# Order of work in the output projection, the gate/up products and the last rows of a decoder block on one core

## The chip, the cores and the metric

The kernel runs on one core of one Trainium2 chip. The metric is device time in microseconds for one launch, the median over the runs shown; lower is better.

## What is computed

The reference is one decoder layer on 1024 tokens of width 1024, in float32: RMSNorm, one projection, two attention branches merged by gates, an output projection, then a SwiGLU feed-forward of width 2816 and a last RMSNorm. The part that matters here, cut from it:

```
merged = (gates[:, :, 0] * (o_a @ w_branch_dsa[l])
          + gates[:, :, 1] * (o_b @ w_branch_diff[l]))
x = x + merged @ w_out[l]

h = rmsnorm(x, norm_ffn_g[l])
gu = h @ w_ffn_in[l]
x = x + (jax.nn.silu(gu[..., :D_FF]) * gu[..., D_FF:]) @ w_ffn_out[l]

return rmsnorm(x, norm_final_g)
```

## The kernel before

Every float32 product is made of three matmuls, with the operands split into a high and a low part (`PASS`: hi·hi, lo·hi, hi·lo). ScalarE (ACT) writes the high part, GpSimd (POOL) or VectorE (DVE) the low part (L101, L102).

**Output projection.** The merged activations come as eight chunks of 128 channels; the last chunk is finished by DVE and ACT just before the projection begins. `outp(q, i)` makes one block of 128 tokens by 256 columns: 24 matmuls (L968) over the eight chunks into a bank `mm`, of which there are two, and then DVE adds the bank to the token row `x2[i]` (L973), which was loaded from memory (L924) into a row tile of the pool `r4`. That pool opens after the pool of the branch stage has closed, on the same bytes.

**Gate and up products.** The 22 column groups f of 128 gate and 128 up channels are made by Strassen's scheme: seven products of 12 matmuls for each f, in the order A11, S2, A12, S3, S1, A22, S4 (`SEQ`). `load_f` brings a gate row and an up row of weights (L936). DVE builds S1 to S4 from them (L1043 to L1046); `prep` splits each operand four products ahead, the high part on ACT (`ahi`) and the low part on POOL (`alo`), with six buffers each. `product_out` takes the results out of the banks. S2, S3 and A22 collect in one bank `tr`: DVE copies out S2's sum (L1088) before S3 may add to it, and S3's (L1094) before A22 may. S4 has the bank `big` (L1105 takes it out, ACT applies SiLU at L1106, L1107 multiplies). After every odd f, `sums` makes four more DVE combinations of the pair (L1119 to L1122) for the down projection and stores them. On even f, `load_w` loads two rows of down weights; on odd f, `tsums` combines them on POOL (L1138 to L1141) and stores them (L1143). The passage from an odd f to the next f is called a seam below.

All loads and stores are issued by one queue, SP, in program order; each waits for its own condition, and what stands behind it waits too. The row tiles r0 to r15 are handed out from a list of free halves (`full`, `half_`), first freed first. The order on each engine is set by a scheduler at compile time, from the program's order and its own estimate of when operands are there; `keep_in_program_order` pins an instruction. Engines run their queues in that order.

**Last rows.** The last three units of the down projection are done row by row: DVE adds the bank to x2 (L1276), ACT squares, and `finish` makes the last norm of the row (L1240, L97, POOL's power at L98, then L1244 on ACT and L1245 on DVE) and stores it (L1247).

```
        product(n)
        prep(n + AHEAD)
        if j == 5:
            load_f(f + 2)
        if j == 3:
            if f % 2 == 0:
                load_w(f // 2)
            else:
                tsums(f // 2)
```

Of the kernel before, what the change touches and what calls it, by code (L numbers as in the profile page):

```python
# [22 lines left out]
KC = D // P  # L23
# [27 lines left out]
def block_kernel(ctx, tc, x, pos, g_mix, w_qk, w_v, q_scale, w_idx, w_gate, ikg, ikb, lams, sub_g, gate_b,  # L51
                 w_bdsa, w_bdiff, w_out, g_ffn, w_ffi, w_ffo, g_fin, out):
    nc = tc.nc
    V, A, G, T = nc.vector, nc.scalar, nc.gpsimd, nc.tensor
# [7 lines left out]
    def mm_bank():  # L62
        return ps.tile([P, 512], F32, name="mm")
# [36 lines left out]
    def split(hi, lo, src, lo_eng):  # L100
        A.activation(hi, src, AF.Copy)  # L101
        lo_eng.tensor_sub(lo, src, hi.bitcast(F32))  # L102
# [356 lines left out]
    for br in range(2):  # L459
        w0 = 8 * br  # L460
        for u in range(2):
            fetch(w0 + 2 + u)
            xx = []
            for c in range(2):
                pt = mm_bank()
# [16 lines left out]
        for c in range(2, 8):  # L482
            fetch(w0 + c + 2)
            for u in range(2):
                pt = mm_bank()
# [8 lines left out]
    for g in range(4):  # L494
        w0 = 16 + 2 * g
        for s in range(4):
            if s % 2 == 0:
                fetch(w0 + 2 + s // 2)
            pt = mm_bank().rearrange("p (a b) -> p a b", a=2)
            for tt in range(2):  # L500
                t = 2 * s + tt
                n = 0
# [298 lines left out]
    for m in range(8):  # L801
        prs = {}
        for j, t in enumerate(ORDER2):
# [6 lines left out]
            n = 8 * m + j  # L810
# [28 lines left out]
    with tc.tile_pool(name="mw", bufs=2) as mw:  # L839
        wot = {}  # L840

        def fetch_o(n, eng=G):
            if n < 8 and n not in wot:
                wot[n] = W3.get(w_out[n // 2, n % 2], eng)
# [25 lines left out]


    R4 = 16
    r4p = ctx.enter_context(tc.tile_pool(name="r4", bufs=1))
    r4p.tile([P, 32], F32, name="shift")
    rows_ = [r4p.tile([P, D], F32, name=f"r{j}") for j in range(R4)]
    b1p = ctx.enter_context(tc.tile_pool(name="b1", bufs=1))
# [1 line left out]
    class Space:  # L878
# [26 lines left out]
        def drop(self, *aps):  # L905
            for ap in aps:
                self.free += self.of.pop(id(ap))[1]
# [4 lines left out]
    def blk(early):  # L912
        if early:
            return b1p.tile([P, 2, 4, 512], F32R, name="blk", bufs=2)
        return b2p.tile([P, 2, 4, 512], F32R, name="blk", bufs=5)
# [16 lines left out]
    def load_f(f):  # L932
        if f < NF and f not in raws:
            raws[f] = [full() for _ in range(2)]
            for j, t in enumerate(raws[f]):
                nc.sync.dma_start(t, w_ffi[f + j * NF])  # L936
# [13 lines left out]
    def turn2(op, p_):  # L950

        pt = big_bank().rearrange("p u (c t) -> p u c t", c=4)
        for u in range(2):
            turn(pt[:, u], 0, tt[p_ + u][op])
        return pt

    def land2(op, p_, pt):
        sl = slice(p_ * P, p_ * P + 2 * P)
        hi, lo = (ops[op][:, a, :, sl].rearrange("p c (u t) -> p u c t", u=2) for a in range(2))
        split(hi, lo, pt, V)  # L960

    def outp(q, i):
        act = actA if i < 4 else actB
        pt = mm_bank()
        n = 0
        for k in range(KC):
            for a, b in PASS:
                T.matmul(pt[:, :256], lhsT=act[a][:, k, i % 4 * P:i % 4 * P + P],  # L968
                         rhs=wot[2 * q + k // 4][b][:, (k % 4) * 256:(k % 4) * 256 + 256],
                         start=n == 0, stop=n == 23)  # L970
                n += 1
        sl = slice(q * 256, q * 256 + 256)
        V.tensor_add(x2[i][:, sl], pt[:, :256], x2[i][:, sl])  # L973

# [18 lines left out]
        d["B22"] = sp4.second(hB)  # L993

    for q in range(2):
        for n in range(NT):
            outp(q, n)
            if q == 1 and n == 0:
                A.activation(small.tile([P, 1], F32, name="warm"), x2[0][:, 256:257], AF.Silu)
            if q == 1 and n in (1, 4):  # L1000
                fetch_o(4 + (n == 4))
# [5 lines left out]
    for n in range(NT + LAG + 1):  # L1007
        if n < NT:
            outp(2, n)
        if n >= LAG and n - LAG < NT:  # L1010
            i = n - LAG
            outp(3, i)
            rows(i)
        if n > LAG:
            i = n - LAG - 1
# [16 lines left out]
    def prep(n, early=False):  # L1032
        if n >= len(plan):
            return
        f, (a_, _, _) = plan[n]
        if f not in src_:
            g, u = raws[f]
            src_[f] = dict(A11=g[:, :512], A12=g[:, 512:], A22=u[:, 512:], own=[g, u])
        d = src_[f]
        if a_[0] == "S" and "S2" not in d:  # L1040
            S1, S2, S4 = (half_() for _ in range(3))
            S3 = u = d["own"][1][:, :512]
            V.tensor_add(S1, u, d["A22"])  # L1043
            V.tensor_sub(S2, S1, d["A11"])
            V.tensor_sub(S3, d["A11"], u)  # L1045
            V.tensor_sub(S4, d["A12"], S2)  # L1046
            d.update(S1=S1, S2=S2, S3=S3, S4=S4)
            d["own"] += [S1, S2, S4]
        if early:
            t = W3.pool.tile([P, 1024], F32R, name="raw", bufs=2)  # L1050
            hi, lo = t[:, :512], t[:, 512:]
        else:
            hi = arp.tile([P, 512], F32R, name="ahi", bufs=6)
            lo = arp.tile([P, 512], F32R, name="alo", bufs=6)
        split(hi, lo, d[a_], G)
        wops[n] = hi, lo
        if a_ == "S4":
            drop(*d["own"])
# [3 lines left out]
    def product(n):  # L1062
        product_mm(n)
        product_out(n)
# [64 lines left out]
    def load_w(j):  # L1129
        wrow[j] = [full() for _ in range(2)]  # L1130
        for q, t in enumerate(wrow[j]):
            tc.keep_in_program_order(nc.sync.dma_start(t, w_ffo[2 * j + q]))
# [34 lines left out]
    def split_u(n):  # L1167
        if n >= len(unit) or n in uop:
            return
        if n % 2 == 0:  # L1170
            ublk[n // 2] = blk(False).rearrange("p a b c -> p (a b c)").rearrange("p (n a c) -> p n a c", n=2, a=2)
        v = ublk[n // 2][:, n % 2]
        split(v[:, 0, :], v[:, 1, :], uraw[n], V)
        drop(uraw[n])
        uop[n] = v
# [18 lines left out]
    for n in range(2, len(plan)):  # L1194
        f, j = n // 7, n % 7
        if f == 0:
            for op in {2: ("T3",), 3: ("T1",), 4: ("T4",), 5: ("B22",)}.get(n, ()):
                ops[op] = blk(False)
                for p_ in (0, 2):
                    land2(op, p_, turn2(op, p_))  # L1200
                drop(*(tt[p_][op] for p_ in range(4)))
                if op == "T3":
                    load_f(1)
        product(n)
        prep(n + AHEAD)
        if j == 5:
            load_f(f + 2)
        if j == 3:
            if f % 2 == 0:
# [3 lines that stand above are left out]
        if f == NF - 1 and j:  # L1213
            for k in (0, 1):
                load_u(2 * j - 2 + k)
                if j > 1:
                    split_u(2 * j - 4 + k)
# [19 lines left out]

    def finish(i):
        sq = sqs[i]
        V.tensor_add(sq[:, 0:1], sq[:, 0:1], sq[:, 1:2])  # L1240
        r = small.tile([P, 1], F32, name="rstd")
        rsqrt(r, sq[:, 0:1], D, EPS)

        A.activation(x2[i][:, :512], x2[i][:, :512], AF.Copy, scale=r)  # L1244
        V.scalar_tensor_tensor(x2[i][:, 512:], x2[i][:, 512:], r, gfin[:, 512:], op0=OP.mult, op1=OP.mult)  # L1245
        for u in range(2):
            nc.sync.dma_start(out[i * P:(i + 1) * P, u * 512:u * 512 + 512], x2[i][:, u * 512:u * 512 + 512])  # L1247

    def evict(p, r, X):
        L, H = slice(0, 512), slice(512, 1024)  # L1250
        if p == 0:
            pA[r] = half_()
            A.activation(pA[r], X, AF.Copy)
        elif p == 1:
            V.tensor_add(x2[r][:, L], X, x2[r][:, L])
            square(r, 0)
            G.tensor_mul(x2[r][:, L], x2[r][:, L], gfin[:, L])
        elif p == 2:
            u2[r] = half_()
            V.tensor_add(u2[r], X, pA[r])  # L1260
            G.tensor_add(u2[r], u2[r], x2[r][:, H])
        elif p == 3:
            u3[r] = half_()
            V.tensor_add(u3[r], X, pA[r])
            G.tensor_add(u3[r], u3[r], x2[4 + r][:, H])
            G.tensor_add(pA[r], pA[r], x2[4 + r][:, L])
        elif p == 4:
            V.tensor_add(x2[4 + r][:, L], X, pA[r])
            square(4 + r, 0)
            G.tensor_mul(x2[4 + r][:, L], x2[4 + r][:, L], gfin[:, L])  # L1270
        elif p == 5:
            V.tensor_add(x2[4 + r][:, H], X, u3[r])
            square(4 + r, 1)
            finish(4 + r)
        else:
            V.tensor_add(x2[r][:, H], X, u2[r])  # L1276
            square(r, 1)
            finish(r)

    def bank_set(k):  # L1280
        if k:
# [16 lines left out]
    for n, (p, j) in enumerate(unit):  # L1298
        if j == 0 and p in OPEN:
            bs_ = bank_set(p == 2)  # L1300
        if n == 2:
            x2_load()
            gfin = row4(g_fin)
        if n < len(unit) - TAILU:
            for r in R:
                unit_mm(n, r)
                if j == NP - 1:
                    evict(p, r, bs_[r])
        elif n == len(unit) - TAILU:
            for r in R:  # L1310
                for m in range(n, len(unit)):
                    unit_mm(m, r)
                evict(p, r, bs_[r])
        split_u(n + SA)
        load_u(n + LA)

# [74 lines left out]
```

## Time and profile before

| | us |
|---|---|
| median of 3 runs (1617.27 to 1619.66) | 1617.34 |
| the profiled execution | 1619.83 |
| its span, first to last instruction | 1617.9 |
| TensorE (PE) busy in the span | 1548.1 |
| DVE busy | 1156.8 |
| ACT busy | 669.1 |
| POOL busy | 568.7 |

The span is that of the profiled execution alone; about 2 us lie outside it. PE, DVE, ACT, POOL and SP are the engines; "idle before, releaser" is how long an engine had nothing to do before an instruction and what ended that. The output projection runs from 843 to 944 us of the span, the gate and up products from 946 to 1395, the down projection from 1395 to 1608, the last rows to the end.

### The profile page before, as it was taken

What the parts mean: (1) busy time and instruction counts of PE and PEld (TensorE: products, weight loads), DVE (VectorE), ACT (ScalarE), POOL (GpSimd) and SP (SyncE); (2) the same over time, 40 slices, a digit from 0 to 9 for tenths busy, and PEclk for the clock granted to TensorE, in tenths of its full rate; (3) what the DMA queues carried; (4) which work ended last, traced back from release to release, by engine and by line L of the source; (5) the groups of instructions that cost most, each with busy time, mean ns of one, the idle gap of its engine ahead of it and who ended that gap; (6) DMA issues with size and microseconds to landing.
All of it is one profiled execution on the core that took longest, in us unless ns stands there. A gap on an engine that the chain in (4) does not pass through costs nothing. (4 is left out here: it accounts for less than half of the span.)

```text
span 1617.9 us, 22643 instructions
## 1 busy us (share of the span) xinstructions
PE 1548.1 (96%) x8204; PEld 1318.3 (81%) x8204; DVE 1156.8 (71%) x1880; ACT 669.1 (41%) x1199; POOL 568.7 (35%) x465
## 2 busy tenths in 40 slices
PE   7999999999999998999999989999999999999997
PEld 6788879998888787788779977788788878887886
DVE  6579999989999999788781486555555555755653
ACT  5454542231221888777730243233233223443343
POOL 2541611242220013322421136666566666203311
PEclk9999999999999999999999999999999999999999
DMA  5243243349421476774474133444344445885532
GB/s 174 86 146 128 88 148 107 111 141 245 137 89 40 105 152 161 186 197 144 153 260 170 53 110 130 149 163 166 133 169 163 159 150 195 315 316 178 166 130 104
DMA packets 108079, 247.45 MB, mean 153 GB/s; under 512 B 12480, under 2 KB 30016, under 8 KB 107968
## 3 DMA queue, kind: packets, MB, share of 16 engines
q1 hardware_dynamic: 107968, 246.02, 46.7%
q8 instruction: 64, 1.05, 0.3%
q14 instruction: 47, 0.39, 0.1%
HBM read 167.06 MB, written 78.91 MB: 152 GB/s over the span
## 5 line engine op out<-in xcount | busy, mean ns | idle before, releaser
L102 POOL TENSOR_TENSOR alo<-r,ahi 128x512 fp32r<-128x512 f32 x152 | 207.2, 1371 | 163.5 <-ACT ahi L101 147.7
L102 POOL TENSOR_TENSOR wlo<-raw,whi 128x1024 fp32r<-128x1024 f32 (+1 forms) x49 | 116.6, 2385 | 288.4 <-ACT whi L101 288.4
L101 ACT ACTIVATE ahi<-r 128x512 fp32r<-128x512 f32 x152 | 95.4, 631 | 260.3 <-PE big L1076 88.1
L1076 PE MATMUL tr<-blk,ahi 128*128 128x512 f32 x528 | 165.6, 394 | 8.0 <-DVE r L1088 7.3
L299 DVE MAX8 m<-score 128x8 f32<-128x640 f32 (+5 forms) x176 | 162.6, 924 | 5.4 <-POOL score L283 0.4
L300 DVE MATCH_REPLACE8 score<-m,score 128x640 f32<-128x640 f32 (+5 forms) x176 | 159.5, 906 | 0.0
L102 DVE TENSOR_TENSOR blk<-r,blk 128x1024 fp32r<-128x1024 f32 x77 | 101.7, 1353 | 73.7 <-ACT blk L101 73.2
L101 ACT ACTIVATE whi<-raw 128x1024 fp32r<-128x1024 f32 (+1 forms) x52 | 53.4, 1031 | 207.1 <-issue 110.2
L1076 PEld LDWEIGHTS tr<-blk,ahi 128*128 128x128 f32 x528 | 99.1, 189 | 32.6 <-DVE r L1088 10.7
L101 ACT ACTIVATE blk<-r 128x1024 fp32r<-128x1024 f32 x77 | 78.1, 1053 | 108.3 <-PE big L1292 44.4
L1076 PE MATMUL big<-blk,ahi 128*128 128x512 f32 x352 | 108.9, 390 | 0.9 <-DVE blk L102 0.9
L427 PE MATMUL mm<-hT_hi,whi 128*128 128x512 f32 x256 | 102.8, 401 | 3.3 <-DVE st_lo L489 2.3
L1076 PE MATMUL mm<-blk,ahi 128*128 128x512 f32 x336 | 104.3, 391 | 0.8 <-ACT r L1085 0.8
L1076 PE MATMUL tr<-blk,alo 128*128 128x512 f32 x264 | 103.7, 393 | 0.6 <-POOL alo L102 0.6
L427 PE MATMUL mm<-hT_lo,whi 128*128 128x512 f32 x256 | 101.2, 395 | 0.0
L427 PE MATMUL mm<-hT_hi,wlo 128*128 128x512 f32 x256 | 101.0, 394 | 0.0
L427 PE MATMUL big<-hT_hi,whi 128*128 128x512 f32 x256 | 99.6, 389 | 0.0
L427 PE MATMUL big<-hT_lo,whi 128*128 128x512 f32 x256 | 99.6, 389 | 0.0
L427 PE MATMUL big<-hT_hi,wlo 128*128 128x512 f32 x256 | 99.6, 389 | 0.0
L1292 PE MATMUL big<-blk 128*128 128x512 f32 x396 | 91.8, 391 | 1.9 <-DVE r L1260 1.5
L1292 PEld LDWEIGHTS big<-blk 128*128 128x128 f32 x396 | 73.8, 188 | 19.5 <-issue 1.9
L1076 PEld LDWEIGHTS big<-blk,ahi 128*128 128x128 f32 x352 | 66.0, 188 | 15.8 <-DVE blk L102 1.7
(286 smaller groups left out, 3965.1 us busy)
## 6 DMA issues: line engine op xcount, KB each, us to landing
r<-in_w_ffi_dram SPq DMA_DIRECT2D x44, 512.0 KB, 4.5
r<-in_w_ffo_dram SPq DMA_DIRECT2D x22, 512.0 KB, 4.8
tdr<-r SPq DMA_DIRECT2D x22, 512.0 KB, 2.6
sdr<-r SPq DMA_DIRECT2D x44, 256.0 KB, 2.6
r<-sdr SPq DMA_DIRECT2D x44, 256.0 KB, 3.9
r<-tdr SPq DMA_DIRECT2D x44, 256.0 KB, 3.9
r<-actdr SPq DMA_DIRECT2D x33, 256.0 KB, 4.0
r<-in_w_ffo_dram SPq DMA_DIRECT2D x33, 256.0 KB, 4.5
```

The costliest lines, as they stand in the source:

```text
L101: A.activation(hi, src, AF.Copy)
L102: lo_eng.tensor_sub(lo, src, hi.bitcast(F32))
L299: tc.keep_in_program_order(V.max(m8, work[t]))
L300: V.match_replace(work[t], m8, work[t], GONE)
L427: T.matmul(dst, lhsT=w[b][:, k * P:(k + 1) * P], rhs=hT[a][:, k, u * 512:(u + 1) * 512], start=n == 0, stop=n == 23)
L1076: T.matmul(banks[z], lhsT=w[b][:, k * P:(k + 1) * P], rhs=o[:, a, k, :], start=first and m == 0, stop=last and m == 11, skip_group_check=True)
L1292: T.matmul(bs_[r], lhsT=v[:, a, r * P:(r + 1) * P], rhs=v[:, b, 512:], start=p in OPEN and j == 0 and m == 0, stop=p in SHUT and j == NP - ...
```

## The change

Four edits. The first two blocks of the output projection are begun with seven of their eight chunks each, and the last chunk of both follows. The pool of row tiles is opened with waits per tile, so that a row tile waits for the last users of its own bytes and not for those of the whole region. `load_f(f + 2)` is called at product 3 of every f but the first, two products sooner. In the last rows, `finish` of a row is called after the next row's eviction, and its first DVE instruction is pinned to program order.

```
-    r4p = ctx.enter_context(tc.tile_pool(name="r4", bufs=1))
+    r4p = ctx.enter_context(tc.tile_pool(name="r4", bufs=1, reuse_waits="tile"))
...
-    def outp(q, i):
+    def outp(q, i, pt=None, ks=range(KC)):
         act = actA if i < 4 else actB
-        pt = mm_bank()
-        n = 0
-        for k in range(KC):
+        pt = mm_bank() if pt is None else pt
+        n = 3 * ks[0]
+        for k in ks:
...
+        if ks[-1] < KC - 1:
+            return pt
...
     for q in range(2):
+        first2 = [outp(0, n, None, range(KC - 1)) for n in range(2)] if q == 0 else []
         for n in range(NT):
-            outp(q, n)
+            if n < len(first2):
+                outp(q, n, first2[n], range(KC - 1, KC))
+            else:
+                outp(q, n)
...
-        if j == 5:
+        if j == (3 if f else 5):
             load_f(f + 2)
...
-        V.tensor_add(sq[:, 0:1], sq[:, 0:1], sq[:, 1:2])
+        tc.keep_in_program_order(V.tensor_add(sq[:, 0:1], sq[:, 0:1], sq[:, 1:2]))
...
             square(r, 1)
-            finish(r)
+            if r:
+                finish(r - 1)
...
                 evict(p, r, bs_[r])
+            finish(3)
```

In the changed file the lines behind the output projection carry numbers 6 higher (L1043 is L1049, L1088 is L1094, L1105 is L1111, L1119 is L1125), and L936 keeps its number.

DVE at the seam from f = 9 to f = 10, before: from S4's eviction of f = 9 (L1105, from a bank `big`) to S2's eviction of f = 10 (L1088, from the bank `tr_11576`). The names r0 to r15 are the row tiles.

```order
L1105 TENSOR_TENSOR r7_8900<-big_11487,r7_8900 128x512
L1107 TENSOR_TENSOR r6_8899<-r6_8899,r4_8897 128x512
L1119 TENSOR_TENSOR r12_8905<-r14_8907,r6_8899 128x512
L1120 TENSOR_TENSOR r15_8908<-r12_8905,r14_8907 128x512
L1121 TENSOR_TENSOR r14_8907<-r14_8907 128x512
L1122 TENSOR_TENSOR r0_8893<-r6_8899,r15_8908 128x512
L1088 TENSOR_TENSOR r1_8894<-tr_11576,r2_8895 128x512
```

The same place with the change; the next row is L1094, S2's eviction of f = 10.

```order
L1049 TENSOR_TENSOR r2_8895<-r15_8908 128x512
L1049 TENSOR_TENSOR r2_8895<-r3_8896 128x512
L1050 TENSOR_TENSOR r7_8900<-r2_8895,r6_8899 128x512
L1111 TENSOR_TENSOR r5_8898<-big_11489,r5_8898 128x512
L1051 TENSOR_TENSOR r3_8896<-r1_8894,r3_8896 128x512
L1051 TENSOR_TENSOR r15_8908<-r6_8899,r15_8908 128x512
L1113 TENSOR_TENSOR r10_8903<-r10_8903,r9_8902 128x512
L1125 TENSOR_TENSOR r9_8902<-r12_8905,r10_8903 128x512
L1050 TENSOR_TENSOR r9_8902<-r2_8895,r1_8894 128x512
L1126 TENSOR_TENSOR r7_8900<-r9_8902,r12_8905 128x512
L1127 TENSOR_TENSOR r12_8905<-r12_8905 128x512
L1128 TENSOR_TENSOR r14_8907<-r10_8903,r7_8900 128x512
```

Sums of weight rows of the next two f (S1, S2, S3, here from the rows r15 and r6 of f = 12 and r3 and r1 of f = 11) now stand in the seam, three of them ahead of S4's eviction and three behind it; before, those of one f stood behind each f's own products.

SP around the stores of the combined down weights of f = 8 and 9 (`tdr4`), before:

```order
L936 DMA r11_8904<-in_w_ffi_dram 128x1024
L1115 DMA actdr8_8936<-r14_8907 128x512
L936 DMA r8_8901<-in_w_ffi_dram 128x1024
L1143 DMA tdr4_0_9002<-r9_8902 128x1024
L1143 DMA tdr4_1_9003<-r10_8903 128x1024
L1116 DMA actdr9_8937<-r6_8899 128x1024
```

and with the change:

```order
L1149 DMA tdr4_0_9002<-r6_8899 128x1024
L1149 DMA tdr4_1_9003<-r15_8908 128x1024
L936 DMA r6_8899<-in_w_ffi_dram 128x1024
L936 DMA r4_8897<-in_w_ffi_dram 128x1024
L936 DMA r15_8908<-in_w_ffi_dram 128x1024
L1138 DMA r13_8906<-in_w_ffo_dram 128x1024
L936 DMA r8_8901<-in_w_ffi_dram 128x1024
```

The gate and up rows r6 and r15 of f = 12 are loaded into the tiles that the two stores ahead of them read; r4 and r8 are the rows of f = 13.

PE at the first two blocks of the output projection (banks `mm_9017` and `mm_9043`, with the change `mm_9039`), where the first matmul of block 0's last chunk stands; before, after seven matmuls of block 1:

```order
L968 MATMUL mm_9043<-whi_8763,actA0_8572 128x256
L968 MATMUL mm_9017<-whi_8804,actA0_8572 128x256
L968 MATMUL mm_9043<-whi_8763,actA1_8573 128x256
L968 MATMUL mm_9043<-wlo_8764,actA0_8572 128x256
L968 MATMUL mm_9043<-whi_8763,actA0_8572 128x256
```

and with the change, after 21 of them:

```order
L968 MATMUL mm_9039<-wlo_8805,actA0_8572 128x256
L968 MATMUL mm_9017<-whi_8804,actA0_8572 128x256
L968 MATMUL mm_9017<-whi_8804,actA1_8573 128x256
L968 MATMUL mm_9017<-wlo_8805,actA0_8572 128x256
L968 MATMUL mm_9039<-whi_8804,actA0_8572 128x256
```

Block 1 has given 14 more of its matmuls to the time ahead of the last chunk.

## Rows read from the trace of the kernel before

**Rows 1.** TensorE's waits over the span (us in total, times, longest).

```profile
PE tr L1076 <- DVE r L1088: 7.3, 8, 2.0
```

**Rows 2.** DVE's waits from 955 to 1400 us.

```profile
DVE r L1043 <- DMA r<-in_w_ffi_dram: 21.6, 14, 2.9
```

**Rows 3.** Chain of waits: single products of 12 matmuls (start, duration).

```profile
1031.18 3.02 PE tr L1076 x12
...
1081.18 2.72 PE mm L1076 x12
...
1089.35 2.72 PE tr L1076 x12
...
1149.19 4.61 PE tr L1076 x12
```

**Rows 4.** TensorE's timeline (start, busy, what; in brackets idle before, releaser).

```profile
1031.18 0.73 PE L1076 MATMUL tr<-blk,ahi 128*128 128x512 f32 x2 [1.91 <-DVE r L1088]
...
1149.19 0.88 PE L1076 MATMUL tr<-blk,ahi 128*128 128x512 f32 x2 [2.02 <-DVE r L1088]
```

**Rows 5.** DVE's timeline, f = 4 to 6.

```profile
1066.96 0.69 DVE L1043 TENSOR_TENSOR r<-r 128x512 f32<-128x512 f32 x1 [2.91 <-DMA r<-in_w_ffi_dram]
...
1081.41 0.68 DVE L1105 TENSOR_TENSOR r<-big,r 128x512 f32<-128x512 f32 x1
1082.79 0.82 DVE L1107 TENSOR_TENSOR r<-r,r 128x512 f32<-128x512 f32 x1 [0.70 <-ACT r L1106]
...
1084.98 1.78 DVE L1121 TENSOR_TENSOR r<-r 128x512 f32<-128x512 f32 x1
...
1087.29 0.68 DVE L1088 TENSOR_TENSOR r<-tr,r 128x512 f32<-128x512 f32 x1
```

**Rows 6.** SP's timeline, the stores of the combined down weights.

```profile
1072.21 3.07 SPq L1143 DMA_DIRECT2D tdr<-r  x2
```

**Rows 7.** Page, part 6: DMA issues, KB each, median us to landing.

```profile
tdr<-r SPq DMA_DIRECT2D x22, 512.0 KB, 2.6
```

**Rows 8.** POOL's timeline in the same stretch.

```profile
1073.63 1.29 POOL L1141 TENSOR_TENSOR r<-r 128x512 f32<-128x512 f32 x1
1074.88 3.78 POOL L102 TENSOR_TENSOR alo<-r,ahi 128x512 fp32r<-128x512 f32 x3
...
1081.76 1.30 POOL L102 TENSOR_TENSOR alo<-r,ahi 128x512 fp32r<-128x512 f32 x1 [1.43 <-ACT ahi L101]
```

**Rows 9.** Time to landing, issues of 1102 to 1103 and 1089.2 to 1093 us.

```profile
r<-in_w_ffi_dram SPq DMA_DIRECT2D x1, 512.0 KB, 3.5
...
r<-in_w_ffi_dram SPq DMA_DIRECT2D x1, 512.0 KB, 7.0
```

**Rows 10.** Busy time by stretch: PE, PEld, DVE, ACT, POOL, granted clock, DMA, GB/s.

```profile
1149.20:1189.80 40.60, 40.34 (x169) 32.88 (x170) 20.93 (x25) 10.88 (x19) 23.36 (x18) 0.96 0.42 149
```

**Rows 11.** Timeline of all engines at the output projection's opening.

```profile
842.48 0.62 PE L631 MATMUL big<-oT_hi,wlo 128*128 128x512 f32 x2
...
848.97 0.59 PE L968 MATMUL mm<-whi,actA 128*128 128x256 f32 x2 [2.51 <-ACT actA L101]
...
849.56 0.68 DVE L102 TENSOR_TENSOR actB<-gt,actB 128x512 fp32r<-128x512 f32 x1
...
850.30 3.75 SPq L924 DMA_DIRECT2D r<-in_x_dram  x8
...
853.68 0.42 DVE L973 TENSOR_TENSOR r<-mm,r 128x256 f32<-128x256 f32 x1 [3.44 <-DMA r<-in_x_dram]
...
854.16 0.50 PE L968 MATMUL mm<-whi,actA 128*128 128x256 f32 x2 [1.04 <-DVE r L973]
```

**Rows 12.** DVE's timeline at the last rows.

```profile
1608.49 0.75 DVE L1245 SCALAR_TENSOR_TENSOR blk<-blk,rstd,r 128x512 f32<-128x512 f32 x1 [0.67 <-POOL rstd L98]
...
1610.83 0.68 DVE L1276 TENSOR_TENSOR blk<-tr,r 128x512 f32<-128x512 f32 x1
...
1613.31 0.75 DVE L1245 SCALAR_TENSOR_TENSOR blk<-blk,rstd,r 128x512 f32<-128x512 f32 x1 [0.67 <-POOL rstd L98]
```

## The prediction

> **What bounds the kernel now.** I read the waits of TensorE first: only a wait of that engine can be won in the three stages that the change touches. In the gate and up products there is one large entry, S3 waiting for DVE to take S2's sum out of the bank [rows 1]. The waits of DVE say why: the sum S1 (L1043) waits for a weight row 14 times [rows 2], and DVE's timeline shows the eviction L1088 standing behind such a wait [rows 5]. The chain of waits gives the price of one product, 2.72 us, and of the first one after a wait, 3.02 [rows 3]: a wait costs its idle time and 0.3 more. After one wait of 2.02 us [rows 4] the first product took 4.61 [rows 3], and the granted clock of that stretch is 0.96 [rows 10]: its first matmuls ran at the lower of the clock's two levels (1.2 and 2.4 GHz), which cost another 1.6.
>
> **The sooner loads: what they remove.** All eight of these waits are in the second f of a pair, where the changed order has no weight sum ahead of L1088, or (in two early and late pairs) one whose row came long before. Removed: 7.3 idle [rows 1], 8 × 0.3 and 1.6 for the clock: 11.3 us. Neither bound is far off: a stray wait may stay, and nothing else is freed there.
>
> **What they move.** The weight sums of two f now stand together in the seam, from S4's eviction L1105 of an odd f to L1088 of the next. I count the instructions in which two operands come from SBUF, as POOL can block those. Before: five between L1105 and L1088, the same at every seam. Changed: in the six seams from f = 7 to f = 18 three ahead of L1105 and eight behind it; at f = 5 three and six; at f = 3 and f = 1 three and seven; the last seam, after f = 19, is as before. So nine seams change. I lay the new order over the seam of f = 5 in the trace. S4 ends at 1081.18, and S3 of the next f is due at 1089.35 [rows 3]. L1105 began at 1081.41 and L1088 ended at 1087.97 [rows 5]: 1.4 us to spare.
>
> First, the start. The first sum ahead of L1105 reads an up row, and that row is loaded into a tile which the second store of the combined down weights must have read. POOL made these weights by 1074.92 [rows 8]; the two stores were issued from 1072.21 to 1075.28, at about 0.33 each [rows 6], so the second at 1074.95; it lands 2.6 later [rows 7], at 1077.55. Ahead of the load in SP's queue stands another row's load, which waits for POOL's split of A12, the second of the three from 1074.88 on [rows 8]: 1077.4. The row is therefore asked for at about 1077.9 and lands 3.5 later when alone [rows 9], at 1081.4; about a microsecond more behind the load ahead of it. At 1081.76 POOL starts a split of 1.3 us [rows 8], and a DVE sum that meets one waits until it ends: L1121, 0.6 alone (the step between free neighbours), took 1.78 [rows 5]. Three sums of 0.6 and one such collision of about 1.2 from 1081.4 end at 1084.4; from the end of the split, 1083.06, at 1084.9. L1105 starts near 1084.6, 3.2 later than before.
>
> Second, behind L1105. Two of the three added sums fill the 0.70 in which DVE waited for SiLU [rows 5]; net 3 × 0.6 − 0.7 = 1.1 without collisions. At the pace of the trace's own run, five in 4.5 us from L1107 to L1088 with one collision [rows 5], net 3 × 0.9 − 0.7 = 2.0. I take 1.55, as POOL goes on with one split per product. L1088 then ends at 1087.97 + 3.2 + 1.55 = 1092.7: **3.4 us late.** With fewer sums behind L1105: 2.6 at f = 5 and at f = 1, 3.3 at f = 3. Part of it shows one product earlier, since ACT's eviction of A11 (which A12 needs) waits behind SiLU; the sum is the same.
>
> Sum of the seams: 6 × 3.4 + 2.6 + 3.3 + 2.6 = 28.9 idle, 9 × 0.3 = 2.7 for restarts. The bounds for one seam: if the row were there in time, the sums could run from 1080.9 and L1105 start 1.3 later, with 1.1 behind it: 1.05 late. If the row lands like the slowest of a queued group, 7.0 [rows 9], L1105 is 5.2 later, with 2.0 behind it: 5.8 late.
>
> **The clock.** A wait of 1.91 us was followed by a product of 3.02, one of 2.02 by 4.61 [rows 3, 4]. All my waits are longer than both, so I take the second row: 9 × 1.6 = 14.4; the first row gives 0, and that is a rival. The Trainium skill ("TensorE: Matmul & The Clock Gate", Part 1, on the HAM clock gate) says that the array is throttled by default and that activity releases it; by that rule a seam that leaves TensorE idle brings the slow stretch back, with the sum above, and without it the sum would be 14.4 lower. The trace agrees at 1149.19 and not at 1031.18.
>
> **The output projection.** TensorE idled 2.51 us for the last chunk and 1.04 for block 0's bank [rows 11]. The bank was late because DVE's L973 waited for its token row, and that load was issued at 850.30 [rows 11]. Its wait is now, by the order, for TensorE's own last use of those bytes, at the latest the end of the branch matmuls, 843.1 [rows 11]: the row lands before 847. L973 is then held only by DVE's own split, which ends at 850.24 [rows 11], so block 2 starts near 850.8 instead of 854.16, 3.4 sooner. Before, seven matmuls of block 1 already stood ahead of the last chunk, so the new opening adds 14 of about 0.12 us, 1.7, and no more. Between 1.7, if the row is no sooner, and 3.4 I take 2.8, as the early loads share the queues with the gate row that the last chunk waits for.
>
> **The last rows.** The eviction of the last row at 1610.83 stood behind the scaling of row 2; now it stands behind that of row 1, which was at 1608.49 [rows 12], so it runs near 1609.1. The last row's own scaling (1613.31) gains less, because the small steps and scaling of row 2 now come between: I get 1612.4, a gain of 0.9, between 0 and 1.7.
>
> **Sum.** 28.9 + 2.7 + 14.4 − 11.3 − 2.8 − 0.9 = **+31.0 us**. The profiled execution took 1619.83, its span 1617.9, the median is 1617.34: 0.15% lower than the profiled one. The difference applies to either; from the median it gives 1648.
>
> **Rivals.**
> - *The seam holds (faster).* If the rows land well before S4 ends and the sums fit into the 1.4 us of slack and SiLU's gap, L1088 is never late: −11.3 − 2.8 − 0.9 = −15.0, 1602. The point is L1088 ending by 1089.35. For it: three sums of 0.6 are short, and the load is called two products earlier. Against it: the second store of the down weights was issued at 1074.95, and 2.6 + 3.5 behind it is 1081.05, with three sums still ahead of L1105. Chance 0.10.
> - *Only the lower bound.* The row is in time and POOL collides little: 9 × (1.05 + 0.3) = 12.2, no drop of the clock, −15.0: 1614.5. Chance 0.10.
> - *Late, at full clock.* The seams are late as worked out, but the clock holds as it did after 1.91 us: +16.6, 1634. For it: A12 runs between the two parts of the wait. Chance 0.25.
> - *Queued loads.* The row lands 7 us after its issue as in a queued group: 9 × (5.8 + 0.3 + 1.6) − 15.0 = +54, 1671. Against it: only one load stands directly ahead. Chance 0.08.
> - That the change does not do what it says holds for the opening alone, whose cover was half there; it is in the term.
>
> **How the numbers follow.** My forecast has 0.47, and 1648 is its time. The range, 1613 to 1664, takes in the full-clock case and the lower bound; left out are the case where the seam holds and the heaviest one. About 0.2% (3.2 us) is what can be told from no change. Faster by more: 0.10, and 0.03 of the lower-bound case; within: 0.07 of it; slower: 0.80. The likeliest sign's own range is 1630 to 1664.
>
> **What would show it.** Right: TensorE's wait of tr L1076 on S2's eviction (now L1094) grows from 7.3 to about 25 to 35 us, at the even f, nine times; DVE waits for a weight row (now L1049) just ahead of S4's eviction in these seams; products of over 4 us follow; the first token row lands before 848, and block 2 starts near 851. Wrong: that wait near zero and seams with L1094 in time, or a row that lands before 1080 on the scale used here. If the waits are there but the first products after them take 3.0, the clock's term was the error.

## The result and the profile after

The changed kernel takes 1670.8 us (median of 4, 1668.93 to 1671.69); the kernel before took 1618.5 (4 runs, 1617.27 to 1623.28). The ratio is 1.031, 95% interval 1.028 to 1.034: slower by 52.3 us, as the sign said, but above the range, which ended at 1664. The span of the profiled execution is 1668.7 against 1617.9: 50.8 more.

The gate and up stage, first product to first matmul of the down projection, took 449.3 us before (945.91 to 1395.25) and takes 503.7 now (943.54 to 1447.20). TensorE's waits in it, changed kernel, 955 to 1450 us:

```profile
PE tr L1082 <- DVE r L1094: 32.6, 9, 4.2
PE mm L1082 <- ACT r L1091: 12.5, 9, 2.4
```

L1094 is S2's eviction, L1088 in [rows 1]; L1091 is ACT's eviction of A11. Nine waits each, 45.1 us together, in the nine passages that the prediction named; the eight waits of 7.3 us in the second f of a pair are gone. One passage in full, f = 9 to 10. First TensorE (start, busy, what, idle before and what ended it):

```profile
1182.75 0.62 PE L1082 MATMUL tr<-blk,ahi 128*128 128x512 f32 x2
...
1184.82 0.73 PE L1082 MATMUL mm<-blk,ahi 128*128 128x512 f32 x2 [1.23 <-ACT r L1091]
...
1191.83 1.22 PE L1082 MATMUL tr<-blk,ahi 128*128 128x512 f32 x2 [3.98 <-DVE r L1094]
```

DVE in the same passage:

```profile
1175.47 0.69 DVE L1106 TENSOR_TENSOR r<-tr,r 128x512 f32<-128x512 f32 x1 [2.03 <-PE tr L1082]
...
1180.60 1.29 DVE L1049 TENSOR_TENSOR r<-r 128x512 f32<-128x512 f32 x2 [3.64 <-DMA r<-in_w_ffi_dram]
1181.81 0.68 DVE L1050 TENSOR_TENSOR r<-r,r 128x512 f32<-128x512 f32 x1
1182.41 0.68 DVE L1111 TENSOR_TENSOR r<-big,r 128x512 f32<-128x512 f32 x1
1183.01 1.28 DVE L1051 TENSOR_TENSOR r<-r,r 128x512 f32<-128x512 f32 x2
1184.22 0.69 DVE L1113 TENSOR_TENSOR r<-r,r 128x512 f32<-128x512 f32 x1
1184.94 1.67 DVE L1125 TENSOR_TENSOR r<-r,r 128x512 f32<-128x512 f32 x1
1186.53 1.78 DVE L1050 TENSOR_TENSOR r<-r,r 128x512 f32<-128x512 f32 x1
1188.23 0.68 DVE L1126 TENSOR_TENSOR r<-r,r 128x512 f32<-128x512 f32 x1
1188.83 0.68 DVE L1127 TENSOR_TENSOR r<-r 128x512 f32<-128x512 f32 x1
1189.43 1.75 DVE L1128 TENSOR_TENSOR r<-r,r 128x512 f32<-128x512 f32 x1
1191.10 0.68 DVE L1094 TENSOR_TENSOR r<-tr,r 128x512 f32<-128x512 f32 x1
```

POOL beside it:

```profile
1184.36 3.40 POOL L102 TENSOR_TENSOR alo<-r,ahi 128x512 fp32r<-128x512 f32 x2 [4.34 <-ACT ahi L101]
1189.13 1.50 POOL L102 TENSOR_TENSOR alo<-r,ahi 128x512 fp32r<-128x512 f32 x1 [1.37 <-ACT ahi L101]
```

And A22's eviction in the passage of [rows 5], before the change:

```profile
1078.50 0.69 DVE L1100 TENSOR_TENSOR r<-tr,r 128x512 f32<-128x512 f32 x1 [2.03 <-PE tr L1076]
```

Read the passage from the top. L1106 evicts A22. Then DVE waits 3.64 us for an up row, for a weight sum of f = 12, while S4's sum stands finished in its bank. The three sums done, S4's eviction L1111 starts 6.94 us after A22's; before it was 2.91 (1078.50 to L1105 in [rows 5]). Behind it stand eight operations, three of them held by POOL's splits (1.67, 1.78, 1.75 instead of 0.68), and S2's eviction starts 8.69 after S4's instead of 5.88 [rows 5]. 4.0 + 2.8, less the 1.4 of slack, is 5.4; TensorE's two waits in this passage are 5.2. Over the nine passages S4's eviction starts 7.10 us after A22's in the mean (2.96 before), and S2's 8.49 after S4's (5.84 before).

The Trainium skill ("SBUF — State Buffer", "SBUF: two separate sides") says that a DVE operation with two inputs from SBUF and a POOL operation that reads SBUF exclude each other for a whole instruction. The trace agrees: the operations with an operand from a PSUM bank stay at 0.68 throughout, and those held, each beside one of the POOL rows above, are 1.0 to 1.1 longer.

SP's queue shows why the row is late; the third of the loads is the row waited for:

```profile
1169.06 3.06 SPq L1149 DMA_DIRECT2D tdr<-r  x2
1172.21 2.90 SPq L936 DMA_DIRECT2D r<-in_w_ffi_dram  x3
```

The times to landing of the four L936 loads of this stretch (minimum, median, maximum):

```profile
DMA to landing us min/median/max: 4.1/4.5/5.8
```

The third load is issued at 1174.7, when the store ahead of it in its tile has landed, and takes the 5.8. The call was moved by two products, this load by more: the scheduler orders SP's queue as well, and it is not the program's order there. The up row of f = 12 was asked for during S3 of f = 10 in the kernel before (1170.07 us) and is asked for during A22 of f = 9 here, five products sooner.

The windows of the same passage (span, busy by engine, granted clock, DMA share, GB/s):

```profile
1184.80:1191.80 7.00, 3.04 (x12) 2.17 (x12) 6.96 (x8) 1.60 (x3) 4.46 (x3) 0.93 0.71 260
1191.80:1197.10 5.30, 5.27 (x12) 4.12 (x13) 1.18 (x2) 0.11 (x1) 0.00 (x0) 0.50 0.13 49
```

The product after the wait runs at 0.50, the lower of the two levels.

The output projection, changed kernel (TensorE, then SP's first load of token rows):

```profile
850.04 0.38 PE L968 MATMUL mm<-whi,actA 128*128 128x256 f32 x1 [0.98 <-ACT actA L101]
...
851.79 0.50 PE L968 MATMUL mm<-whi,actA 128*128 128x256 f32 x2 [0.17 <-DVE r L975]
```

```profile
842.77 4.61 SPq L924 DMA_DIRECT2D r<-in_x_dram  x8
```

From the last chunk to block 2: 1.75 us, where it was 5.19 [rows 11]; the token rows are asked for 7.5 us sooner. The last rows, DVE:

```profile
1660.89 0.68 DVE L1282 TENSOR_TENSOR blk<-tr,r 128x512 f32<-128x512 f32 x1
...
1664.17 0.75 DVE L1251 SCALAR_TENSOR_TENSOR blk<-blk,rstd,r 128x512 f32<-128x512 f32 x1 [0.66 <-POOL rstd L98]
```

Measured from the start of the down projection the last eviction comes 1.9 us sooner and the last scaling 1.1 [rows 12].

### The profile page after: what moved, and what is told of

Same layout as the page of the kernel before. It is cut to its first block, busy times and chain, and to the rows that moved or that the text cites. A ratio compares the mean times of both kernels' runs of the same rounds, so it can differ in the third digit from the quotient of the medians.

```text
span 1668.7 us, 22638 instructions
## 1 busy us (share of the span) xinstructions
PE 1564.9 (94%) x8204; PEld 1328.3 (80%) x8204; DVE 1158.4 (69%) x1880; ACT 667.8 (40%) x1199; POOL 561.3 (34%) x465
## 3 DMA queue, kind: packets, MB, share of 16 engines
q8 instruction: 64, 1.05, 0.3%
## 5 line engine op out<-in xcount | busy, mean ns | idle before, releaser
L1082 PE MATMUL tr<-blk,ahi 128*128 128x512 f32 x528 | 176.4, 416 | 33.1 <-DVE r L1094 32.6
L1082 PEld LDWEIGHTS tr<-blk,ahi 128*128 128x128 f32 x528 | 105.6, 202 | 59.9 <-DVE r L1094 36.6
L1082 PE MATMUL mm<-blk,ahi 128*128 128x512 f32 x336 | 106.1, 397 | 12.5 <-ACT r L1091 12.5
L1082 PE MATMUL tr<-blk,alo 128*128 128x512 f32 x264 | 109.1, 413 | 0.6 <-POOL alo L102 0.6
L1082 PEld LDWEIGHTS mm<-blk,ahi 128*128 128x128 f32 x336 | 63.0, 189 | 29.0 <-ACT r L1091 16.3
```

Of the source, the lines that this page charges most:

```text
L1082: T.matmul(banks[z], lhsT=w[b][:, k * P:(k + 1) * P], rhs=o[:, a, k, :], start=first and m == 0, stop=last and m == 11, skip_group_check=True)
```

## The experiments

Ratios are against the kernel before, run on the same chip between them.

**The parts of the change.** The late load: the changed kernel with one line set back.

```diff
-        if j == (3 if f else 5):
+        if j == 5:
```

> The changed kernel with the gate and up rows loaded where they were (in the sixth product of every f); the other three edits stay. Seam theory (all of the loss is made in the nine passages from an odd f to the next, by the order of the weight sums that the sooner loads bring): the two gains that stand in the trace of the changed kernel are left, 2.4 in the output projection and 1.15 behind the gate and up stage: 1618.5 - 3.5 = 1615.0. Rival (the new waits of the row tiles, or an earlier start of the stage, have a part in the loss): above 1620.

Measured: 1616.15 us, ratio 0.9989 (0.9975 to 1.0004); its stage takes 449.6 us. The loss is gone, and the interval holds 0.9978, which the two gains would give (1615.0 of 1618.5). It holds 1 as well, so the times alone do not show these gains; the trace does, with 1.75 us again from the last chunk to block 2 and 1.1 less from the first matmul of the down projection to the end. The sooner loads alone, in the kernel before:

```diff
-        if j == 5:
+        if j == (3 if f else 5):
```

> The kernel before with nothing but the sooner loads. Seam theory: the gate and up stage takes the 54.3 us more that it took in the trace of the changed kernel: 1618.5 + 54.3 = 1673, with TensorE's wait for S2's eviction near 32 us. Rival (the row tiles' own waits, which this kernel does not have, are needed for the loss): 1640 or less.

Measured: 1672.45 us, ratio 1.0336 (1.0314 to 1.0358), waits 35.3 (S3) and 8.7 (A12). The whole loss is this one line's; the row tiles' own waits have no part.

**Row late, or chain long?** First the row sooner, in the order of the changed kernel:

```diff
-        for t, dr in zip((w0, w1), t_dr[j]):
+        for t, dr in zip((w0, w0), t_dr[j]):
```

> The changed kernel, with both stores of the combined down weights taken from the first row of the pair, so that the tile of the second row is free as soon as POOL is done with it and the up row is asked for some 2 us sooner and as the first of the loads; T2 and T4 of the down projection are then not the right ones. DVE's order is that of the changed kernel, word for word. Row theory (the late row makes the whole wait): nothing is left of the 45 us of waits in the nine passages, nor of what follows them: about 1607. Both parts (row late, and eight operations behind S4's eviction where there were five): the row is 2 to 4 us sooner, the waits fall from 5.0 to between 1.0 and 3.0 for each passage: 1630 to 1653. Order alone: 1671, no change.

Measured: 1655.99 us, ratio 1.0223 (1.0198 to 1.0248). TensorE's waits, 955 to 1450 us:

```profile
PE tr L1082 <- DVE r L1094: 34.2, 9, 4.2
...
PE mm L1082 <- ACT r L1091: 0.5, 1, 0.5
```

The stage is 491.2 us, 12.5 less than in the changed kernel: the wait of A12 is gone, that of S3 untouched. DVE shows why that is all, one passage:

```profile
1172.10 0.69 DVE L1106 TENSOR_TENSOR r<-tr,r 128x512 f32<-128x512 f32 x1 [2.03 <-PE tr L1082]
...
1174.77 2.43 DVE L1049 TENSOR_TENSOR r<-r 128x512 f32<-128x512 f32 x2 [1.19 <-POOL alo L102]
...
1177.73 0.68 DVE L1111 TENSOR_TENSOR r<-big,r 128x512 f32<-128x512 f32 x1
...
1186.41 0.68 DVE L1094 TENSOR_TENSOR r<-tr,r 128x512 f32<-128x512 f32 x1
```

No wait for a row, yet L1111 is still 5.63 behind A22's eviction, as three sums and a split of POOL are ahead of it, and L1094 is 8.68 behind L1111, as before. Row theory and order alone both fall. The expectation of both parts was 3 us too low at its end, and its waits of 1.0 to 3.0 were too short: 3.9 us a passage are left. Then the chain shorter, with the sooner loads kept:

```diff
-            if f % 2:
+            if f == NF - 1:
                 sums(f // 2)
...
         product(n)
+        if j == 1 and f and f % 2 == 0:
+            sums(f // 2 - 1)
```

S2's eviction and the first activation sum also keep the order in which they are written; the scheduler then spreads the weight sums somewhat differently too.

> The changed kernel, sooner loads kept, with the four sums of the activations written behind S2's eviction of the next f and held there. The sum that waits for a row still stands ahead of S4's eviction in most passages, but between that eviction and S2's there are two to four operations instead of eight. Both parts (row late, chain behind S4's eviction): S2's eviction comes 5 us sooner after S4's, so the wait of S3 (about 4.0 in each passage) goes, that of A12 (1.2 to 2.4) stays, at its price without the long drop of the clock: 1670.8 - 36 - 10 to 20 = 1615 to 1625. Row theory: 1655 or more, since the row is as late as ever.

Measured: 1624.58 us, ratio 1.0042 (1.0028 to 1.0055); the stage is 458.8, 44.9 less. Its waits, 955 to 1410 us (L1100 is S3's eviction):

```profile
PE tr L1082 <- DVE r L1094: 6.5, 8, 2.6
PE mm L1082 <- ACT r L1091: 4.6, 6, 1.6
PE tr L1082 <- DVE r L1100: 3.9, 6, 0.7
```

The two runs do not part the loss cleanly. 12.5 and 44.9 together are 57.4, more than the 54.0 by which the changed kernel's stage is longer than with the late load. In this run the start moved too: S4's eviction is 5.86 us behind A22's in the mean of the nine passages, against 7.10 in the changed kernel; the sum ahead of it waits for a row in six of them, and the passage after f = 15 has the order of before. The run with the sooner row parts it better. Of the 4.1 us by which S4's eviction starts later in the changed kernel than before, 1.6 go with the row's wait (5.46 behind A22's there); 2.5 stay, and so do the 2.7 behind that eviction. Both parts count, and the order is the heavier.

**Are sooner loads bad in themselves?** The weight sums pinned where they are written, behind S1's eviction:

```diff
-            V.tensor_add(S1, u, d["A22"])
+            tc.keep_in_program_order(V.tensor_add(S1, u, d["A22"]))
...
-            V.tensor_add(ev["u2"], X, ev["u2"])
+            tc.keep_in_program_order(V.tensor_add(ev["u2"], X, ev["u2"]))
```

(the other three sums likewise)

> The changed kernel, loads as soon as there, but the four weight sums and S4's eviction keep the order in which they are written, so that all four sums of the next f stand behind S1's eviction and none in the passage between two f. Seam theory: no waits in the passage and none in the second f of a pair either: 1615.0 - 11.3 = 1603.7, up to 1610 if the four sums in a row hold the evictions behind them up. Rival (the sooner loads cost by themselves, by the queues and the transfers that they meet, whatever DVE's order): 1650 or more.

Measured: 1631.99 us, ratio 1.0081 (1.0058 to 1.0103): neither. S3 still waits ten times, 17.7 us. POOL and DVE at one of these passages, with no weight sum in it:

```profile
1153.56 1.29 POOL L1147 TENSOR_TENSOR r<-r 128x512 f32<-128x512 f32 x1
1158.86 11.04 POOL L102 TENSOR_TENSOR alo<-r,ahi 128x512 fp32r<-128x512 f32 x7 [4.00 <-ACT ahi L101]
```

```profile
1163.69 1.67 DVE L1125 TENSOR_TENSOR r<-r,r 128x512 f32<-128x512 f32 x1
1165.40 1.67 DVE L1126 TENSOR_TENSOR r<-r,r 128x512 f32<-128x512 f32 x1
1166.98 1.78 DVE L1127 TENSOR_TENSOR r<-r 128x512 f32<-128x512 f32 x1
1168.68 1.76 DVE L1128 TENSOR_TENSOR r<-r,r 128x512 f32<-128x512 f32 x1
1170.36 0.68 DVE L1094 TENSOR_TENSOR r<-tr,r 128x512 f32<-128x512 f32 x1
```

The sums come late, the splits that need them bunch, seven in a row, and each of the four activation sums meets one. So the next kernel writes them two products sooner, in a function of their own (wsums, the code of the sums taken out of prep), pinned with the evictions of S2 and S4:

```diff
         product(n)
+        if f and f + 1 < NF and j == 2:
+            wsums(f + 1)
```

> The changed kernel, loads as soon as there, with the four weight sums of the next f written and held directly behind S2's eviction, two products sooner than in the kernel of the pinned sums; the evictions of S2 and S4 are held as well. If the pinned sums lost their time because they came too late, so that POOL's splits bunched and met all four activation sums: no waits in either passage now, 1615 less the 8.9 us of waits and some 4 of restarts and clock, 1602 to 1607. If the sooner loads cost by themselves, 1630 as with the pinned sums.

Measured: 1606.65 us (6 runs, 1604.34 to 1609.8), ratio 0.9932 (0.9919 to 0.9946). The stage takes 440.2. Of TensorE's waits from 957 to 1400 us one is left (L1109 is S3's eviction in this file):

```profile
PE tr L1091 <- DVE r L1109: 1.0, 1, 1.0
```

One product later:

```diff
-        if f and f + 1 < NF and j == 2:
+        if f and f + 1 < NF and j == 3:
```

> As the one before, with the four sums behind S3's eviction, one product later. If lateness of the sums is what counts: between 1604 and 1632, nearer to the first, as the splits have one product less of lead. If it is not: the same as the one before.

Measured: 1610.32 us, ratio 0.9954 (0.9941 to 0.9967), ten waits of 0.34 to 0.46: lateness of the sums counts. And the sums behind S2's eviction with the loads as before the change:

```diff
-        if j == (3 if f else 5):
+        if j == 5:
```

> The kernel with the sums directly behind S2's eviction, with the loads in the sixth product, as before the change. If a late row is harmless where its sum stands behind S2's eviction (S3's eviction has a product of slack): within 3 us of the one with the sooner loads. If the sooner loads are what makes that order possible: the sums wait for their rows and hold S3's eviction up, 1612 or more.

Measured: 1606.32 us, ratio 0.9933 (0.9918 to 0.9947). The same. Both beat both kernels, and it is the order, not the sooner loads, that does it: against the late load in the scheduler's order (0.9989) it is worth 0.6%.

**Half of the edit.** Sooner in odd f alone, and, in a second kernel, one product sooner:

```diff
-        if j == (3 if f else 5):
+        if j == (3 if f % 2 else 5):
```

```diff
-        if j == (3 if f else 5):
+        if j == (4 if f else 5):
```

> The changed kernel with the sooner loads in the odd f alone; the even f keep the sixth product. By DVE's order no weight sum is left between S4's eviction of an odd f and S2's of the next beyond those of the kernel before, and in the passage from even to odd the sum that waits for a row stands ahead by a whole f. Seam theory: no wait of the size of the changed kernel, and most of the 8.9 us of waits in the odd f gone with their restarts: 1605 to 1613. Rival (any sooner load costs, by transfers and splits that bunch): above 1625.

> The changed kernel with the loads one product sooner than before (fifth instead of sixth) and not two. DVE's order at the passage from odd to even f is that of the kernel before; at the passage from even to odd the first two sums still stand about S4's eviction, their row asked for 2.7 us sooner. Seam theory: no loss, and the waits of the odd f (8.9 us in eight, 3.2 at most) vanish or nearly so: 1604 to 1612. Rival (sooner loads cost in proportion to how much sooner they are): near 1643, half of the loss.

Measured: 1622.6 us, ratio 1.0025 (1.0012 to 1.0039), and 1620.48, ratio 1.0017 (1.0002 to 1.0032). No rival's loss, but none of the gain that I expected of either. The waits only changed places, odd f alone, 955 to 1400 us (L1103 is S1's eviction):

```profile
PE big L1082 <- DVE r L1103: 7.1, 2, 3.6
PE mm L1082 <- ACT r L1091: 2.7, 7, 0.5
PE tr L1082 <- DVE r L1094: 1.5, 6, 0.3
```

11.3 us, where the kernel of the late load has 8.9; one product sooner has 9.0. Why their medians are a few us above that of the late load, at nearly the same waits, is not settled; the trace of the first is of its fastest execution (1617.9 us, of 12 up to 1627.12), so what the others lost is not in it.

**The opening.** Each half of it without the other, in the kernel of the late load, one run each; first the opening without the tiles' own waits, then those without the opening:

```diff
-    r4p = ctx.enter_context(tc.tile_pool(name="r4", bufs=1, reuse_waits="tile"))
+    r4p = ctx.enter_context(tc.tile_pool(name="r4", bufs=1))
```

```diff
-        first2 = [outp(0, n, None, range(KC - 1)) for n in range(2)] if q == 0 else []
+        first2 = []
```

> The kernel of the late load without the row tiles' waits for their own bytes: the opening of two blocks of seven chunks alone (and the last rows). From the arrival of the last chunk to the first product of block 2 it was 5.2 us before and 1.75 with both edits. By the prediction's bounds 14 of the 21 chunk products are moved ahead, 1.7 us: 3.5 without the tiles' own waits. If the bank of block 0 is still held by its late token row: 3.5 plus a wait of 1 or more.

> The kernel of the late load without the opening of two blocks: the row tiles wait for their own bytes alone (and the last rows). From the arrival of the last chunk to the first product of block 2 it was 5.2 us before, 5.2 with the opening alone, 1.75 with both. If the tiles' waits take only the 1.04 of the bank away: 4.1, and the opening is worth the other 2.4 once the bank is free. If the tiles' waits are the whole gain: 1.75.

The times, 1614.73 and 1618.61 us, tell nothing: single runs, where the kernel before spreads over 8 us. From the last chunk to block 2 the traces have 5.23 us with the opening alone, and 3.9 with the tiles' own waits alone, where 4.1 was expected. Opening alone, TensorE and DVE:

```profile
849.31 0.38 PE L968 MATMUL mm<-whi,actA 128*128 128x256 f32 x1 [0.50 <-ACT actA L101]
...
854.54 0.80 PE L968 MATMUL mm<-whi,actA 128*128 128x256 f32 x2 [3.66 <-DVE r L975]
```

```profile
854.06 0.42 DVE L975 TENSOR_TENSOR r<-mm,r 128x256 f32<-128x256 f32 x1 [3.48 <-DMA r<-in_x_dram]
```

The tiles' own waits alone, TensorE:

```profile
850.75 0.50 PE L968 MATMUL mm<-whi,actA 128*128 128x256 f32 x2 [2.77 <-ACT actA L101]
...
854.63 0.54 PE L968 MATMUL mm<-whi,actA 128*128 128x256 f32 x2
```

Alone the opening wins nothing: what it saves it waits for at the bank. Alone the tiles' own waits win 1.3. Together they win 3.4. The clock has a part in this. TensorE's longest wait here is 2.51 us before the change, 3.66 with the opening alone and 2.77 with the tiles' own waits alone, and the granted clock behind it is 0.53, 0.51 and 0.59; with both it is 0.98, and the clock stays at 1.00. Before the change, with the slow products inside the interval:

```profile
849.00:852.60 3.60, 3.60 (x18) 3.60 (x19) 1.24 (x2) 0.44 (x1) 0.00 (x0) 0.53 0.37 108
```

## Why the prediction missed its range

- **What bounds, and which passages: right.** Nine passages, the ones named, with a row's wait ahead of S4's eviction. The eight old waits went, as worked out.
- **"L1088 then ends … 3.4 us late": too small, and this is the step that failed.** Both of its terms were. The start was put 3.2 later and was 4.0: the row was asked for when expected (1077.8 on the prediction's scale) but landed 5.8 us after its issue, at 1083.6, not 1081.4; that the three sums met no split here gave some of it back. The sums behind S4's eviction were put at 1.55 and cost 2.8: three met a split of POOL, where I had averaged over a stretch with one. The waits are 45.1 in all, 5.0 a passage, for 28.9: 16.2 of the miss. The lower bound had the same fault: with the row in time S4's eviction was to start 1.3 later and a passage to lose 1.05; with the sooner row it started 2.5 later and a passage lost 3.9.
- **"9 × 1.6" for the clock and "9 × 0.3" for restarts: right in kind, 4 us short.** The products after the long wait of each passage take 4.39 to 5.29 from start to start (mean 4.83 of nine; 2.72 when free): 19.0. Four of them take 5.28 and run at 0.50 throughout, where the row that I took had only its first matmuls slow. The second wait of eight passages adds 0.3 each. Together 21.4, forecast 17.1.
- **Full clock: false here.** All nine passages show a slow product. But the reason given, that these waits were longer than 2.02, was not enough (see the last section).
- **Output projection, −2.8:** the interval it speaks of became 3.4 shorter. In the balance of the two traces 2.4 is left, since the last chunk came 1.1 later. The stated lower bound of 1.7, "if the row is no sooner", was wrong: without the sooner row the gain is nothing. The products behind the last chunk were put at 0.12 us each; before the change they ran 0.21 apart, at the lower clock, a term that the prediction did not have.
- **Last rows, −0.9:** 1.1.
- **Balance:** stage +54.3 from the end of the output projection on, −2.4, −1.1: 50.8, the difference of the spans.

The rival of the queued loads, 1671, hit the time with a landing of 7 us and 2.0 behind S4's eviction; the landing was 5.8 and the chain 2.8. It was right by a sum, not by its mechanism; a chance of 0.08 for it was too low. The range should have reached it, since [rows 9] had shown 7.0 for a load asked for beside others.

## What to carry to other kernels

Loading sooner is no gain by itself: a scheduler that sees data sooner may move the work on it sooner too, in front of work that somebody waits for. Look at what is queued behind each wait on an in-order engine, and write that order by hand where a stage has little slack; here this was worth 0.6% at the same loads (0.9933 against 0.9989), and with the sooner loads it gave the same time. Two edits that free the same step must be judged together: the opening was worth nothing until the bank behind it was free.

## What the runs showed of the hardware

The length of TensorE's wait does not tell by itself whether the clock falls. With the pinned sums the ten waits are all 1.76 to 1.78 us, yet the products after them take 2.85 and 4.2 in turn. With the late load a wait of 3.18 was followed by a product of 2.86, and one of 2.00 by 4.18; with the sooner loads in odd f alone two waits of 3.57 were followed by 2.85 and 2.89. The pinned sums after a wait of 1.76 and one of 1.78 (columns as above, clock third from the end):

```profile
1130.90:1133.80 2.90, 2.86 (x13) 2.37 (x14) 0.00 (x0) 0.00 (x0) 0.00 (x0) 1.00 1.02 345
1171.10:1175.30 4.20, 4.20 (x12) 3.32 (x13) 0.00 (x0) 0.00 (x0) 0.00 (x0) 0.65 0.90 348
```

And odd f alone after one of the waits of 3.57:

```profile
1114.40:1117.30 2.90, 2.83 (x12) 2.36 (x13) 1.91 (x4) 0.00 (x0) 0.00 (x0) 1.00 0.00 0
```

What decides between them these rows do not show.
